# TensorE's order in the strand-only loops follows the kernel's rough clock

## The chip, the cores and the metric

The kernel runs on one core of one Trainium2 chip. The metric is the device time of one execution, in microseconds (us). The engines are named as the profile names them: PE is TensorE (PEld its weight loads), DVE is VectorE, ACT is ScalarE, POOL is GpSimd, SP is SyncE, whose queue issues most DMAs.

## What is computed

Two model blocks run one after the other on 512 latent tokens ("l") and 256 context tokens ("c") of width 1024, in float32. The part that the change touches is the first mixer, `mixer_ab`: a projection, a spatial gate, and a two-directional delta-rule scan over 8 heads of 64.

```python
def rwkv7_scan(r, w, k, v, kk, b, s0):
    def step(s, inp):
        r_t, w_t, k_t, v_t, kk_t, b_t = inp
        sa = jnp.einsum('bhvk,bhk->bhv', s, kk_t)
        s = s * w_t[:, :, None, :] - sa[..., None] * b_t[:, :, None, :] + v_t[..., None] * k_t[:, :, None, :]
        return s, jnp.einsum('bhvk,bhk->bhv', s, r_t)
...
def mixer_ab(hc, hl, ...):
    pc, pl = hc @ w_in, hl @ w_in
    bc, bl = rwkv_bidir(pc, pl, ...)            # both directions, context first
    yl = jnp.concatenate([spatial_gate(pl, a_ws, a_bs, a_gv), bl], axis=-1) @ w_out
    yc = jnp.concatenate([spatial_gate(pc, ...), bc], axis=-1) @ w_out
```

After it come a convolutional feed-forward, a second layer with an mLSTM mixer, and a second block of two hybrid layers (gated delta rule, long convolution, gates) with a last norm.

## The kernel before, in words

Activations lie with channels on the partitions. Large products are split into a high and a low part and done as three matmuls per 128 x 128 weight tile (`mmacc`: L331, L334, L335). The kernel is written for a scheduler that places every engine's instructions by a simulated time; what the kernel's text fixes on top of that is TensorE's order, by "pins".

**Strands.** The scans are Python generators, called strands. `background` adds one; each `yield a, b` says that the piece just written takes `a` ns of TensorE and that the strand can go on about `b` ns later. The kernel keeps a rough clock `now`, advanced by the `a` of every piece and by the matmuls of `mmacc`; a strand is due at `now + b * LF * slow` with LF = 2.5 (`step`). `tick` runs every strand that is due. So the text of the program comes out in the order of the rough clock.

**Pins.** `pin` orders a TensorE instruction behind the one pinned last, without a semaphore. `step` pins the first TensorE instruction of each strand step, and `mmacc` pins the first of its three matmuls while strands are there. A step's other TensorE instructions are not pinned.

**Where only strands run.** `finish(strands)` lets the strands run on, with no large matmul between, until the given ones are done (`wait` moves the rough clock to the next due time). Here the kernel before switches pins off, and forgets the last pinned instruction: the scheduler alone orders TensorE. There are two long such loops, both in `mixer_ab`. The first (`K.finish(early)`) follows `gate_part` and runs until head pairs 0 and 1 are done; pairs 2 and 3 (`rwkv_pair`, one strand per pair) and `ada` run beside them. The rough clock goes from 174 to 466 us there. Then `gemm_out` multiplies by `ab_w_out` with the remaining strands between its matmuls, and `K.drain()` is the second loop, for the last pairs: 532 to 602 us of the rough clock. `hybrid` has a `K.drain()` too, which finds two short steps left.

**Names.** L1025 are the LoRA products of `rwkv_prep` ("wd", then "ad"), L1122 its key products, L1144 the product behind them, L726 and L735 the two half-steps of `Chunk.inverse`, L1177 the products of `rwkv_scan`, L978, L979, L966, L971 those of `rwkv_end`. `ada` multiplies by the `ada_w` weights (L545), eight steps per round, one yield of 860 and 2800 each. The tail of `gate_part`, per segment, is L361 (column sums), L353 on POOL (the root), L375 (broadcast), L1258 on DVE, L1261 (transpose), L1263 on ACT, L1266 (the spatial product), L1269 and L1271 on DVE. PSUM has eight banks; the tail of `gate_part` and `ada` both use bank 3 alone.

Of the kernel before, what the change touches and what calls it, by code (L numbers as in the profile page):

```python
# [81 lines left out]
class Kern:  # L82
# [67 lines left out]

    def finish(self, strands):

        self.pinning, self.pinned = False, None
        while any(s in self.back for s in strands):
            self.wait()
        self.pinning = True

    def wait(self):
        self.now = max(self.now, min(s[2] for s in self.back))
# [2130 lines left out]
```

## Time and profile before

| | |
|---|---|
| median of 3 runs | 3410.71 us (3401.76 to 3412.95) |
| profiled execution | 3407.66 us, span 3406.0 us |
| PE busy | 3156.2 us, 93% of the span |
| DVE busy | 2114.3 us, 62% |
| ACT busy | 1271.8 us, 37% |
| mean granted PE clock | 0.958 |

PE is the busiest engine over the whole. Busy time of PE counts a matmul up to its modelled end, so that short waits between matmuls don't show as idle. The two strand-only loops are short stretches: by the instructions that belong to them, the first has its TensorE work between 374.6 and 711.4 us, the second between 804.7 and 847.8 us of the span.

### The profile page before, as it was taken

What the parts mean: (1) busy time and instruction counts of PE and PEld (TensorE: products, weight loads), DVE (VectorE), ACT (ScalarE), POOL (GpSimd) and SP (SyncE); (2) the same over time, 40 slices, a digit from 0 to 9 for tenths busy, and PEclk for the clock granted to TensorE, in tenths of its full rate; (3) what the DMA queues carried; (4) which work ended last, traced back from release to release, by engine and by line L of the source; (5) the groups of instructions that cost most, each with busy time, mean ns of one, the idle gap of its engine ahead of it and who ended that gap; (6) DMA issues with size and microseconds to landing.
All of it is one profiled execution on the core that took longest, in us unless ns stands there. A gap on an engine that the chain in (4) does not pass through costs nothing. (4 is left out here: it accounts for less than half of the span.)

```text
span 3406.0 us, 61963 instructions
## 1 busy us (share of the span) xinstructions
PE 3156.2 (93%) x25042; PEld 2473.4 (73%) x25042; DVE 2114.3 (62%) x4318; ACT 1271.8 (37%) x2681; POOL 624.0 (18%) x762
## 2 busy tenths in 40 slices
PE   7999988889899999989888999989999998899998
PEld 4878766667588888868766788857667676766756
DVE  4444556545855555584766675668578666777765
ACT  4333333333432222355534332352333335244332
POOL 4111223211000000010010000005158100515700
PEclk9999999999899999989999999989999898999989
DMA  7432545441222122222222233232223253223333
GB/s 233 137 94 71 166 148 166 133 124 51 76 72 69 64 79 66 77 66 71 87 66 87 87 100 123 87 100 72 72 90 100 76 174 95 75 69 100 100 118 105
DMA packets 313570, 336.10 MB, mean 99 GB/s; under 512 B 26542, under 2 KB 259132, under 8 KB 313284
## 3 DMA queue, kind: packets, MB, share of 16 engines
q1 hardware_dynamic: 311172, 329.69, 30.6%
q8 instruction: 197, 3.23, 0.4%
q0 software_dynamic: 2112, 2.45, 0.3%
q14 instruction: 89, 0.73, 0.1%
HBM read 282.13 MB, written 49.94 MB: 97 GB/s over the span
## 5 line engine op out<-in xcount | busy, mean ns | idle before, releaser
L331 PE MATMUL mm<-hl,wh 128*128 128x512 f32 (+1 forms) x3296 | 1252.2, 384 | 53.8 <-DVE qkv L1779 13.8
L334 PE MATMUL mm<-hl,wh 128*128 128x512 f32 (+1 forms) x3296 | 1223.6, 372 | 1.9 <-DVE hl L474 1.6
L335 PE MATMUL mm<-hl,wl 128*128 128x512 f32 (+1 forms) x3296 | 1215.9, 371 | 0.0
L331 PEld LDWEIGHTS mm<-hl,wh 128*128 128x128 f32 x3296 | 629.6, 192 | 194.8 <-issue 40.4
L335 PEld LDWEIGHTS mm<-hl,wl 128*128 128x128 f32 x3296 | 630.3, 191 | 114.0 <-issue 2.3
L334 PEld LDWEIGHTS mm<-hl,wh 128*128 128x128 f32 x3296 | 632.2, 192 | 104.9 <-DVE hl L474 4.0
L77 ACT ACTIVATE wh<-wr 128x512 fp32r<-128x512 f32 (+3 forms) x718 | 367.4, 561 | 698.1 <-PE mm L334 610.9
L78 DVE TENSOR_TENSOR wl<-wr,wh 128x512 fp32r<-128x512 f32 (+3 forms) x718 | 438.3, 644 | 213.6 <-ACT wh L77 196.8
L1357 DVE SCALAR_TENSOR_TENSOR cv<-mm,vecs,cv 128x441 f32<-128x441 f32 (+2 forms) x352 | 243.0, 692 | 94.2 <-ACT cv L1345 88.1
L1408 POOL MEMSET gwh<- 128x1024 f32 x3 | 2.9, 955 | 971.3 <-PE mm L334 971.3
L1779 DVE SCALAR_TENSOR_TENSOR cfa<-ld,vecs,cfa 128x497 f32<-128x497 f32 (+14 forms) x160 | 154.3, 964 | 18.3 <-ACT cfa L1773 16.1
L1945 POOL TENSOR_SCALAR tap<-ld,vecs 128x498 f32<-128x498 f32 (+4 forms) x80 | 150.7, 1883 | 46.7 <-DVE kq L2004 10.4
L1380 DVE TENSOR_TENSOR fy<-fy,mm 128x512 f32<-128x512 f32 x96 | 55.1, 576 | 126.3 <-PE mm L335 125.5
L1946 POOL TENSOR_TENSOR cfa<-cfa,tap 128x498 f32<-128x498 f32 (+4 forms) x80 | 113.0, 1413 | 5.3
L2121 ACT ACTIVATE u<-ps,beT 64x128 f32<-64x128 f32 x128 | 46.3, 362 | 137.1 <-DVE u L2120 136.1
L730 ACT ACTIVATE pad<-ps 128x256 f32<-128x256 f32 (+1 forms) x100 | 46.6, 467 | 129.9 <-PE ps L726 129.4
L1359 ACT ACTIVATE cv<-cv,vecs 128x256 f32<-128x256 f32 (+1 forms) x66 | 43.0, 653 | 132.1 <-DVE cv L1357 77.2
L736 DVE TENSOR_TENSOR cut<-cut,ps 128x256 f32<-128x256 f32 x120 | 49.4, 413 | 58.9 <-PE ps L735 57.2
L353 POOL TENSOR_TENSOR rs<-var,mhalf 128x4 f32<-128x4 f32 (+1 forms) x26 | 28.1, 1082 | 287.5 <-DVE var L351 287.4
L412 PE MATMUL ps<-sq,one 128*128 128x512 f32 (+1 forms) x132 | 64.5, 625 | 17.0 <-ACT sq L382 15.7
L1363 DVE TENSOR_TENSOR cv<-cv,mm 128x512 f32<-128x512 f32 x66 | 39.4, 599 | 65.5 <-ACT cv L1359 36.2
L2120 DVE TENSOR_SCALAR u<-ps,kdT 64x128 f32<-64x128 f32 x128 | 44.6, 348 | 52.9 <-PE ps L2116 44.5
(479 smaller groups left out, 4465.3 us busy)
## 6 DMA issues: line engine op xcount, KB each, us to landing
ar<-in_ada_w_dram SPq DMA_DIRECT2D x96, 512.0 KB
wr<-in_ffn_up_dram SPq DMA_DIRECT2D x44, 1024.0 KB
wr<-in_w_in_dram SPq DMA_DIRECT2D x28, 1024.0 KB
ld<-sp SPq DMA_DIRECT2D x84, 256.0 KB
wr<-in_w_in_dram SPq DMA_DIRECT2D x32, 512.0 KB
xsp<-x SPq DMA_DIRECT2D x48, 256.0 KB
x<-xsp SPq DMA_DIRECT2D x48, 256.0 KB
wr<-in_ffn_down_dram SPq DMA_DIRECT2D x20, 512.0 KB
```

Of the source, the lines that this page charges most:

```text
L77: nc.scalar.activation(h[:, q:e], src, AF.Copy)
L78: nc.vector.tensor_tensor(l[:, q:e], src, h[:, q:e].bitcast(F32), SUB)
L331: mm = nc.tensor.matmul(ps[:m, :n], wh[:, i, :m], H[:, :n], start=first and i == 0, stop=False)
L334: nc.tensor.matmul(ps[:m, :n], wh[:, i, :m], L[:, :n], start=False, stop=False)
L335: nc.tensor.matmul(ps[:m, :n], wl[:, i, :m], H[:, :n], start=False, stop=last and i == nk - 1)
L412: self.nc.tensor.matmul(ps[:, :n], self.one2, t[:, :n], start=first, stop=last)
L736: nc.vector.tensor_tensor(Wp, Wp, ps, SUB)
L1357: nc.vector.scalar_tensor_tensor(t3[:, ro, co], a3[:, ri, ci], tap(ky, kx, ff), t3[:, ro, co], MUL, ADD)
L1380: nc.vector.tensor_tensor(y[s][q], y[s][q], pss[s][:, :n], ADD)
L1779: nc.vector.scalar_tensor_tensor(dst[:, a:b], src[:, a + o:b + o], taps[j], dst[:, a:b], MUL, ADD)
L1945: nc.gpsimd.tensor_scalar(x[:, a:b], src[:, a + o:b + o], taps[j], None, MUL)
L1946: nc.gpsimd.tensor_tensor(g[:, a:b], g[:, a:b], x[:, a:b], ADD)
```

## The change

The two lines that switch pins off and on in `finish` go. Pins then hold in the strand-only loops as they do elsewhere, and the last pinned instruction is kept across the call: the first step in the loop stands behind the last pinned matmul ahead of it, and the first matmul of `gemm_out` behind the last step of the loop.

```diff
     def finish(self, strands):
 
-        self.pinning, self.pinned = False, None
         while any(s in self.back for s in strands):
             self.wait()
-        self.pinning = True
 
     def wait(self):
```

Line numbers below `finish` are two lower in the changed kernel (L545 is L543, L966 is L964, and so on). What the kernel computes, and the text order of its instructions, stay the same. What moves is the place of instructions on the engines.

The first place is TensorE at the start of the first loop, in the kernel before. L361, L375, L1261, L1266 are the tail of `gate_part`, the rest are strand steps; ps_4259 is `ada`'s first bank.

```order
L361 MATMUL ps_4185<-ones_77,sq_4183 128x1 x2
L726 MATMUL ps_4267<-cut_1168,pad_1296 64x64 x8
L726 MATMUL ps_4279<-cut_1543,pad_1644 64x64 x8
L735 MATMUL ps_4291<-pad_1295,bk_3503 64x64 x8
L1177 MATMUL ps_4311<-cut_1163,rk_3652 64x64
```

Sixty rows on, still of the kernel before, `ada` begins, with three of its steps in one piece:

```order
L1177 MATMUL ps_4831<-cut_1538,cut_1542 64x64 x4
L545 MATMUL ps_4259<-ar_4260,csil_341 32x512 x4
L545 MATMUL ps_4259<-ar_4330,csil_341 32x512 x4
L545 MATMUL ps_4259<-ar_4506,csil_341 32x512 x2
L545 MATMUL ps_4259<-ar_4507,csil_341 32x512 x2
```

TensorE at the same place in the changed kernel:

```order
L373 MATMUL ps_4194<-ident_72,rs_4192 128x128 x4
L1259 MATMUL ps_4200<-ident_72,gv_4025 128x128 x4
L1264 MATMUL ps_4207<-wsT_2624,gvt_4205 128x128 x4
L359 MATMUL ps_4220<-ones_77,sq_4218 128x1 x2
L1023 MATMUL ps_4359<-wd_665,up_4337 64x128 x2
L373 MATMUL ps_4227<-ident_72,rs_4225 128x128 x2
L1023 MATMUL ps_4427<-ad_725,up_4337 64x128 x2
L1259 MATMUL ps_4231<-ident_72,gv_4027 128x128 x2
L1264 MATMUL ps_4236<-wsT_2624,gvt_4234 128x128 x2
L543 MATMUL ps_4259<-ar_4260,csil_341 32x512 x4
L724 MATMUL ps_4267<-cut_1168,pad_1296 64x64 x8
L724 MATMUL ps_4279<-cut_1543,pad_1644 64x64 x8
```

The strand steps that stood between the parts of the tail now stand behind `ada`'s first step, and that one behind the whole tail, whose bank it takes.

The second place is TensorE inside the first loop, around an end step of pair 1 (`rwkv_end`: ps_7303, then ps_7346), in the kernel before:

```order
L978 MATMUL ps_7303<-y_1291,heads_87 128x256
L979 MATMUL ps_7303<-bon_1293,heads_87 128x256
L545 MATMUL ps_6451<-ar_7309,csil_341 32x512 x4
L735 MATMUL ps_7336<-cut_4243,bk_6603 64x64 x2
L726 MATMUL ps_7353<-cut_4256,cut_4252 64x64 x8
L966 MATMUL ps_7346<-blk_83,bon_1293 128x2 x2
```

And in the changed kernel:

```order
L976 MATMUL ps_7303<-y_1291,heads_87 128x256
L977 MATMUL ps_7303<-bon_1293,heads_87 128x256
L543 MATMUL ps_6451<-ar_7309,csil_341 32x512 x4
L733 MATMUL ps_7316<-cut_4251,bk_6816 64x64 x8
L733 MATMUL ps_7326<-pad_1643,bk_6422 64x64 x8
L733 MATMUL ps_7336<-cut_4243,bk_6603 64x64 x8
L964 MATMUL ps_7346<-blk_83,bon_1293 128x2 x2
```

One `ada` step and two pieces of other strands' half-steps stood between ps_7303 and ps_7346; now one `ada` step and three whole half-steps do.

## Rows read from the trace of the kernel before

**Rows 1.** The page's first line, of the whole execution.

```profile
span 3406.0 us, 61963 instructions
```

**Rows 2.** Stretches: length, busy PE, PEld, DVE, ACT, POOL, clock, DMA share, GB/s.

```profile
374.67:397.08 22.41, 18.45 (x366) 15.09 (x365) 12.99 (x36) 11.89 (x35) 6.36 (x12) 0.93 0.41 121
397.08:711.40 314.32, 274.06 (x5551) 207.23 (x5551) 190.06 (x486) 117.45 (x359) 88.11 (x157) 0.92 0.51 163
804.70:851.20 46.50, 37.99 (x655) 29.94 (x655) 27.82 (x73) 13.88 (x40) 10.96 (x15) 0.93 0.07 21
110.00:374.00 264.00, 263.92 (x2991) 213.66 (x2990) 119.69 (x266) 100.80 (x227) 49.32 (x88) 1.00 0.33 100
```

**Rows 3.** Timeline of PE, start of the first loop: start, length, instruction, idle before.

```profile
374.17 0.50 PE L361 MATMUL ps<-ones,sq 128*128 128x1 f32 x4
...
376.82 0.65 PE L375 MATMUL ps<-ident,rs 128*128 128x128 f32 x4
...
378.48 0.66 PE L1261 MATMUL ps<-ident,gv 128*128 128x128 f32 x4
...
380.67 1.16 PE L1266 MATMUL ps<-wsT,gvt 128*128 128x128 f32 x8
...
382.75 0.61 PE L361 MATMUL ps<-ones,sq 128*128 128x1 f32 x4
...
387.92 0.43 PE L375 MATMUL ps<-ident,rs 128*128 128x128 f32 x2
...
389.83 0.44 PE L1261 MATMUL ps<-ident,gv 128*128 128x128 f32 x2
...
393.52 0.85 PE L1266 MATMUL ps<-wsT,gvt 128*128 128x128 f32 x4 [2.59 <-ACT gvt L1263]
...
397.08 4.59 PE L545 MATMUL ps<-ar,csil 128*32 128x512 f32 x24
```

**Rows 4.** Timelines of POOL, DVE and ACT around the same tail.

```profile
374.95 1.01 POOL L353 TENSOR_TENSOR rs<-var,mhalf 128x4 f32<-128x4 f32 x1 [2.54 <-DVE var L351]
397.70 0.61 POOL L914 DMA_DIRECT2D up<-in_b_w_up_dram  x1 [3.44 <-DVE gv L1271]
377.58 0.75 DVE L1258 SCALAR_TENSOR_TENSOR gv<-gv,vecs,ps 128x512 f32<-128x512 f32 x1 [0.60 <-PE ps L375]
381.87 0.69 DVE L1269 TENSOR_TENSOR gv<-ps,bs 128x512 f32<-128x512 f32 x1 [1.07 <-PE ps L1266]
395.32 0.41 DVE L1269 TENSOR_TENSOR gv<-ps,bs 128x256 f32<-128x256 f32 x1
379.18 0.60 ACT L1263 ACTIVATE gvt<-ps 128x512 f32<-128x512 f32 x1 [0.54 <-PE ps L1261]
```

**Rows 5.** Waits of PE, 397.2 to 702 us: total, times, longest.

```profile
PE ps L735 <- ACT cut L730: 4.8, 3, 3.6
PE ps L966 <- ACT bon L981: 3.0, 1, 3.0
PE ps L1177 <- DVE cut L1196: 2.8, 3, 2.1
...
PE ps L1025 <- ACT cut L1027: 1.9, 4, 1.0
PE ps L1177 <- ACT Pb L1191: 1.8, 2, 1.4
```

**Rows 6.** Timelines of PE and ACT: a LoRA pair in the first loop.

```profile
386.86 0.45 PE L1025 MATMUL ps<-wd,up 64*64 64x128 f32 x8 [0.67 <-DMA up<-in_b_w_up_dram]
387.36 0.62 ACT L1027 ACTIVATE cut<-ps,hv 128x128 f32<-128x128 f32 x2 [0.84 <-PE ps L1025]
```

**Rows 7.** Timeline of PE: an end step, and what stands inside it.

```profile
574.73 0.70 PE L978 MATMUL ps<-y,heads 128*128 128x256 f32 x2 [1.22 <-ACT cut L1027]
...
576.95 0.63 PE L726 MATMUL ps<-cut,cut 64*64 64x64 f32 x16
580.59 0.61 PE L966 MATMUL ps<-blk,bon 128*128 128x2 f32 x4 [3.01 <-ACT bon L981]
```

## The prediction

> **What bounds the kernel now.** I read the page first: one core, a span of 3406.0 us [rows 1], and PE as the engine that is nearly always busy. Then the stretches. Where large matmuls run beside strands, PE has no idle time at all: 263.92 of 264.00 us busy, at the full granted clock [rows 2]. There pins can only change which work comes first. In the two strand-only loops this is different. From 397.08 to 711.40 us PE is busy for 274.06 of 314.32 us, so 40.3 us are idle, and the clock is 0.92; from 804.70 to 851.20 us it is 37.99 of 46.50 us, so 8.5 us idle at 0.93 [rows 2]. DVE is at 190 of 314 us and ACT at 117, so no engine is full: four strands and `ada` share PE, each waits for its own chain over DVE and ACT, and PE waits when the next instruction in its order isn't ready. The list of waits shows how that is made up: no wait is frequent, each kind comes one to four times with at most 3.6 us [rows 5]. The reader is to see that the change has some 360 us to act on, a tenth of the span, that about 49 us of it are idle PE, and that everything outside can only shift.
>
> What the change does there is to replace one fixed order by another. PE takes its instructions in order in both kernels; no strand can overtake at run time. The question is which order guesses better when a step is ready: the scheduler's simulated time, or the rough clock with its waits of 2.5 times the written latency.
>
> **The change part by part.**
>
> *Start of the first loop.* `ada`'s first step needs bank 3, which the tail of `gate_part` holds until DVE's L1269 has read it, at 395.32 + 0.41 = 395.73 us [rows 4]; `ada` starts at 397.08 [rows 3]. Before, strand steps fill that time. After, the first pinned step of the loop is `ada`'s, and every strand step stands behind it. Between the end of L361 (374.17 + 0.50 = 374.67) and 397.08 PE is busy for 18.45 of 22.41 us [rows 2]; the tail's own pieces are 0.65 + 0.66 + 1.16 + 0.61 + 0.43 + 0.44 + 0.85 = 4.80 [rows 3], so 13.65 us are strand work that moves behind `ada`. But the tail gets quicker when it is alone. Its first half is 0.28 until the root on POOL starts, 1.01 for the root, 0.65 on PE, 0.75 DVE, 0.66 PE, 0.60 ACT, 1.16 PE, 0.69 DVE = 5.80 [rows 3, 4]; the second half, with the first half's durations where no row of its own stands, 0.61 + 0.28 + 1.01 + 0.43 + 0.75 + 0.44 + 0.60 + 0.85 + 0.41 = 5.38. With some 14 hand-offs of about 0.1 (L1261 starts 0.15 after DVE's L1258 ends, ACT's L1263 0.04 after L1261) that is 12.6 us, so `ada` starts near 387.3, 9.8 us sooner, with 13.65 us undone: **+3.9**. The bounds are +13.65 (the tail as slow as now) and 0 (the moved work falls into later idle time). Moved along with it are the weights of pair 3: POOL issues them once the tail's last DVE step has freed their page, at 397.70 [rows 4]; they come sooner by the same 10 us, and no queue is behind in a way that costs.
>
> *The clock there.* A mean of 0.93 over 22.41 us is 14% of the time at the lower of the two levels, 3.1 us [rows 2]. PE will be mostly idle for 12 us, so I expect one more such stretch behind it; half of its work is lost: **+1.6**, bounds 0 and +5.
>
> *LoRA pairs.* From the first "wd" product (386.86) to the end of ACT's tanh (387.36 + 0.62 = 387.98), on which "ad" waits for its bank, 1.12 us pass [rows 6]. The rough clock gives about the same, 0.25 + 0.3 * 2.5 = 1.0 to 1.15 us, in which the changed order has about one piece of another strand, 0.6 us long as the half-step at 576.95 [rows 7]. Sixteen such pairs stand in the loop: 16 * 0.5 = 8.0, less the 1.9 us that PE waits there today [rows 5]: **+6.1**, bounds 0 and +8.
>
> *End steps.* Here the rough clock guesses better. L978 to L966 took 5.86 us, with PE idle for 3.01 at the end [rows 7]. Before, one `ada` step and part of two half-steps stand inside; after, `ada` and three half-steps, about 1 us more of cover. That makes the 3.0 us some 2, and a little at the other five end steps: **-2**, bounds -4 and +2.
>
> *Scan and inverse steps.* In the scan PE waits in five rows, from 2.8 to 1.8 us, 11.5 in all [rows 5]. The rough clock allows 1.6 to 2.0 us for a step, and the order before had put what it took to be ready between them. I take a third more: **+4**. The bounds are wide, since neither order knows how long DVE's queue is: all of 11.5 us gone, or as much again. The inverse half-steps (4.8 us of waits on ACT in three, nearly all one case of 3.6 [rows 5]) I leave as they are, 0.
>
> *The second loop* has 8.5 us idle [rows 2] and two or three strands whose rough waits are all too long by the same factor, so that their order among each other hardly moves: **+1**, bounds -4 and +4. *The joint with `gemm_out`*: its first matmul now stands behind the loop's last step. That is the step that makes its last operand, so I take 0, at most +3. *The drains in `hybrid`* hold two short steps: 0.
>
> The sum is 3.9 + 1.6 + 6.1 - 2 + 4 + 1 = +14.6 us. Against its own time the profiled execution goes from 3407.66 to 3422.3 us; it lies 3.05 us below the median of the runs shown, 3410.71, so the median would be 3425.3. I forecast 3425. A later end of the first loop passes on in full, since behind it stands work that keeps PE full.
>
> **The rivals.** *Faster: the rough clock covers waits better.* Its waits are 2.5 times the written latency, so it puts more work between two steps of a strand than a scheduler that trusts its own shorter times. L966 speaks for it [rows 7]; LoRA pairs and the start speak against. If half of the 40.3 idle us goes, that is -20. With it goes clock: 0.92 over 314.32 us is 16%, 50 us at the lower level, which costs 25 us of work; half of that back is -12. With +3.9 at the start: -28, 3383 us. The Trainium skill (Perfetto Trace Analysis, Matmul Optimizations) says that matmuls should be issued back to back in batches since the engine's clock goes with its use; the changed order does have longer batches, with each step's matmuls less mixed with those of others. The trace agrees in that the full stretch has 1.00 and the loops 0.92 and 0.93 [rows 2]; by that rule alone the 25 us would come back, 3386 us.
>
> *No change.* The idle time moves, its sum doesn't: strands wait for DVE and ACT whatever PE's order, and the start costs 4 us. That gives 3405 to 3420, say 3413. For it speaks that no kind of wait dominates [rows 5]. It is also what would come if the pins changed too little, since a pin holds only the first matmul of a step.
>
> *Much slower: blocked behind DVE's queue.* One wait of 3.6 us shows what happens when ACT or DVE is late and PE's next piece needs it [rows 5]. The scheduler's order hides most such cases by mixing steps; with pins in step order the whole of PE stands. If this comes once in each of some 15 blocks of 128 tokens in the loop, with 2.5 us, that is +37, with the 14.6 above +52: 3462 us. It decides where the delay is longer than the two or three pieces, about 2 us, that stand between.
>
> **How the numbers follow.** The forecast gets 0.42, the faster case 0.18, no change 0.28, much slower 0.12. A measurement of this kernel can tell about 0.3%, 10 us, from no change. Of the forecast's 0.42 a part of 0.08 lies under 10 us. So faster 0.17 (0.01 of the faster case is too small to see), same 0.28 + 0.08 + 0.01 = 0.37, slower 0.34 + 0.12 = 0.46. The forecast alone has 3413 to 3445. The range for eight in ten must reach into both ends: 3388 to 3460.
>
> **What would show it.** The first L543 of `ada` near 387 us with PE idle around the tail of `gate_part`, and strand steps only behind it: the first term. Waits of L1023 on ACT's tanh, short and about sixteen: the third. A shorter wait at L964: the fourth. Idle PE time of the first loop of 50 us or more against 44 says slower, under 30 says faster, and the clock in it goes the same way. The stretches of `gemm_out` and behind the mixer should keep their length; if they change by more than 5 us, something moved that I don't see. The forecast is wrong if DVE's or ACT's order changes so that strands get their results sooner: then all waits shrink together.

## The result and the profile after

The changed kernel takes 3454.94 us (median, 3450.47 to 3464.73), the kernel before beside it 3411.83 us: a ratio of 1.0134 with a 95% interval of 1.0117 to 1.015, that is 43 us more. I had forecast 3425, so the sign was right and the size a third of what came. The first profiled execution of the changed kernel lies 9.8 us above its median. A second one, beside the experiments, took 3450.58 us (median there 3451.28, ratio 1.0128, 1.011 to 1.0146), and all readings below are of that one unless another is named. It stands 42.9 us above the profiled execution of before.

The stretches of the changed kernel, with the columns of [rows 2]: the tail of `gate_part` from the end of its column sums to `ada`'s first product, the first loop, `gemm_out`, the second loop, and all that follows.

```profile
375.21:391.15 15.94, 8.66 (x37) 5.93 (x36) 3.36 (x7) 1.86 (x5) 2.89 (x4) 0.59 0.36 114
391.15:743.40 352.25, 298.83 (x5857) 228.70 (x5857) 199.45 (x514) 132.08 (x392) 90.51 (x167) 0.87 0.48 147
743.40:839.20 95.80, 91.92 (x1015) 71.57 (x1014) 34.49 (x88) 28.27 (x77) 12.31 (x20) 0.96 0.30 90
840.10:887.40 47.30, 39.41 (x652) 33.13 (x650) 25.75 (x66) 13.07 (x38) 11.19 (x15) 0.85 0.06 19
887.40:3440.20 2552.80, 2387.49 (x14012) 1873.52 (x14010) 1678.61 (x3259) 952.65 (x1851) 412.92 (x336) 0.96 0.28 87
```

The last three of these in the kernel before:

```profile
711.40:803.90 92.50, 88.10 (x1000) 68.82 (x997) 34.78 (x88) 29.51 (x81) 13.18 (x21) 0.96 0.29 89
804.70:847.80 43.10, 36.85 (x652) 29.24 (x651) 25.33 (x66) 13.25 (x39) 10.96 (x15) 0.96 0.07 23
847.80:3397.70 2549.90, 2385.63 (x14010) 1874.80 (x14010) 1678.75 (x3259) 952.94 (x1851) 411.23 (x336) 0.96 0.28 87
```

| stretch | before | after | difference | predicted |
|---|---|---|---|---|
| tail of `gate_part` | 22.41 | 15.94 | -6.5 | -9.8 |
| first loop | 314.32 | 352.25 | +37.9 | +23.4 |
| `gemm_out` | 92.50 | 95.80 | +3.3 | 0 |
| second loop | 43.10 | 47.30 | +4.2 | +1 |
| behind | 2549.90 | 2552.80 | +2.9 | 0 |

(The predicted 23.4 of the first loop is the 13.65 us of moved work, 1.6 of clock, and 6.1 - 2 + 4.) Tail and loop together are 31.5 us longer. PE is busy for 8.66 + 298.83 = 307.49 us in them against 18.45 + 274.06 = 292.51 [rows 2], 15.0 more for the same instructions, and idle for 60.7 against 44.2, 16.5 more. The granted clock of the loop is 0.87 where it was 0.92.

The tail, PE's timeline (columns as in [rows 3]):

```profile
376.56 0.65 PE L373 MATMUL ps<-ident,rs 128*128 128x128 f32 x4 [1.35 <-POOL rs L351]
378.12 1.11 PE L1259 MATMUL ps<-ident,gv 128*128 128x128 f32 x4 [0.91 <-DVE gv L1256]
379.92 2.07 PE L1264 MATMUL ps<-wsT,gvt 128*128 128x128 f32 x8 [0.69 <-ACT gvt L1261]
382.78 1.01 PE L359 MATMUL ps<-ones,sq 128*128 128x1 f32 x4 [0.78 <-DVE gv L1267]
386.36 0.69 PE L1023 MATMUL ps<-wd,up 64*64 64x128 f32 x4 [2.57 <-DMA up<-in_b_w_up_dram]
...
391.15 1.94 PE L543 MATMUL ps<-ar,csil 128*32 128x512 f32 x8 [0.52 <-DVE gv L1267]
393.02 1.97 PE L724 MATMUL ps<-cut,pad 64*64 64x64 f32 x32
```

The waits that I had listed are there, and `ada` does stand behind the tail, with nearly all strand steps behind it. Two things are new against [rows 3]. The pieces take nearly twice as long (L1264 2.07 us for 1.16), since the clock is at the lower of its two levels through most of it. And a LoRA step of pair 2, L1023, waits 2.57 us for its weights in the middle of the tail, with the tail's second half behind it in PE's order. POOL issues these weights only behind the second segment's column sums (L359), and that segment's root (L351) stands behind the issues, as POOL's timeline shows:

```profile
384.09 0.62 POOL L912 DMA_DIRECT2D up<-in_b_w_up_dram  x1 [7.58 <-PE ps L359]
...
385.26 0.72 POOL L351 TENSOR_TENSOR rs<-var,mhalf 128x2 f32<-128x2 f32 x1
```

In the kernel before the same product starts at 386.86, also behind a wait for the weights [rows 6], but strand steps fill most of the time ahead of it.

PE's waits in the first loop (total, times, longest), which answer to [rows 5]:

```profile
PE ps L733 <- ACT cut L728: 7.9, 4, 5.5
PE ps L724 <- DVE cut L734: 7.3, 6, 2.8
PE ps L1023 <- ACT cut L1025: 7.0, 7, 3.5
PE ps L1120 <- DVE kq L1101: 6.2, 4, 1.9
PE ps L1175 <- DVE cut L1194: 4.7, 4, 3.2
PE ps L724 <- ACT cut L1151: 4.2, 1, 4.2
PE ps L1175 <- DVE cut L1207: 4.1, 4, 1.5
PE ps L964 <- ACT cut L979: 2.0, 1, 2.0
PE ps L1175 <- DVE cut L734: 1.8, 1, 1.8
PE ps L1175 <- ACT cut L1193: 1.4, 2, 0.9
```

Two rows of the kernel before that [rows 5] left out, of the same list over 397 to 711.4 us:

```profile
PE ps L726 <- DVE cut L736: 2.3, 3, 1.3
...
PE ps L1122 <- DVE kq L1103: 1.7, 3, 1.1
```

So these two rows of waits for DVE, on L734 (its L736) and on L1101 (its L1103), grew from 4.0 to 13.5 us. All waits for DVE in the two lists grew less, from 19.4 to 25.6 us, those for ACT from 17.3 to 25.9, and the longest ones are for ACT. Two of them show how PE comes to stand. Before 424.95 PE waits for L734, which DVE takes up only when it is through with a row of one block's `rwkv_prep` work, of which the last is L1101; before 709.80 it waits for L728, which stands in ACT's queue behind a reload of `gemm_out` that hasn't landed (DVE's timeline, and PE's):

```profile
423.18 1.29 DVE L1101 TENSOR_TENSOR kq<-kq,cut 128x256 f32<-128x256 f32 x2
424.39 0.41 DVE L734 TENSOR_TENSOR cut<-cut,ps 128x256 f32<-128x256 f32 x1
```

```profile
424.95 0.62 PE L724 MATMUL ps<-cut,pad 64*64 64x64 f32 x14 [2.81 <-DVE cut L734]
...
709.80 1.12 PE L733 MATMUL ps<-cut,bk 64*64 64x64 f32 x16 [5.53 <-ACT cut L728]
```

ACT's timeline ahead of the second:

```profile
708.40 1.08 ACT L309 ACTIVATE hl<-ld 128x512 fp32r<-128x512 f32 x2 [4.71 <-DMA ld<-sp]
709.39 0.36 ACT L728 ACTIVATE cut<-ps 128x256 f32<-128x256 f32 x1
```

These waits look like the answer. But the experiments that took some of them away gained little.

### The profile page after: what moved, and what is told of

The parts are those of the page before. It is cut to its first block, busy times and chain, and to the rows that moved or that the text cites. A ratio compares the mean times of both kernels' runs of the same rounds, so it can differ in the third digit from the quotient of the medians.

```text
span 3463.0 us, 61943 instructions
## 1 busy us (share of the span) xinstructions
PE 3192.6 (92%) x25042; PEld 2498.9 (72%) x25042; DVE 2113.3 (61%) x4318; ACT 1275.6 (37%) x2681; POOL 625.0 (18%) x762
## 5 line engine op out<-in xcount | busy, mean ns | idle before, releaser
L728 ACT ACTIVATE pad<-ps 128x256 f32<-128x256 f32 (+1 forms) x100 | 46.6, 467 | 139.5 <-PE ps L724 137.9
L734 DVE TENSOR_TENSOR cut<-cut,ps 128x256 f32<-128x256 f32 x120 | 49.2, 413 | 61.7 <-PE ps L733 60.5
L351 POOL TENSOR_TENSOR rs<-var,mhalf 128x4 f32<-128x4 f32 (+1 forms) x26 | 28.9, 1111 | 290.5 <-DVE var L349 290.4
```

The costliest lines, as they stand in the source:

```text
L734: nc.vector.tensor_tensor(Wp, Wp, ps, SUB)
```

## The experiments

The changed kernel again, for the second profile used above:

> The changed kernel once more, for a second profile of it (the first one's execution lies 9.8 us above its median). Theory (the 9.5 us by which the work behind the mixer was longer in the first profile belong to that execution, not to the change): behind the second loop the two kernels take the same time within 3 us, and loop 1 ends 30 to 36 us later than in the kernel before; 3455 us. Rival (the change also lengthens what comes behind the mixer): 5 us or more are lost there again.

Behind the second loop it takes 2552.80 us against 2549.90, 2.9 more. The first profile had lost some 10 us there, of which 7 were that execution's own.

**Which loop.** Pins in the first loop only, and in the second only:

```diff
     def drain(self):
 
+        self.pinning, self.pinned = False, None
         self.finish(list(self.back))
+        self.pinning = True
```

> Pins stay on in the first strand-only loop and are off in K.drain(), as in the kernel before. Theory (the first loop carries the loss: start, waits, and more time at the lower clock): its loop 1 ends as in the changed kernel, near 749 us of the span, gemm_out keeps its 97 us, the second loop goes back from 47 to about 43 us: 3450 us, +39 on the kernel before. Rival (the second loop's own order costs nothing; what it lost it inherits from the first, by DVE and ACT work that is late): the second loop stays at 47 us, 3455 us. Second rival (the loss is spread evenly by idle time, 40 us in the first loop to 8.5 in the second): 3412 + 43 * 40/49 = 3447 us.

```diff
+    K.pinning, K.pinned = False, None
     K.finish(early)
+    K.pinning = True
```

> Pins are off in the first strand-only loop, as in the kernel before, and stay on in K.drain(). Theory (first loop carries the loss): loop 1 ends near 711 us and gemm_out takes 92.5 us as in the kernel before, the second loop takes 47 us for 43: 3416 us. Rival (the second loop's extra time is inherited from the first): 3412 us, second loop 43 us. Second rival (spread evenly by idle time): 3412 + 43 * 8.5/49 = 3419 us.

The first loop alone gives 3449.95 us, a ratio of 1.011 (1.0093 to 1.0128), +39; the second alone 3411.72, 1.0009 (0.9998 to 1.0019), no difference that can be told. Its interval ends at +6.5 us, though, and its profile has 46.9 us for the second loop against 43.1, so a cost of some 4 us isn't excluded. The loss is made in the first loop, or at its ends.

**The start.** `ada`'s steps without pins, so that strand steps may stand between the parts of the tail again:

```diff
-            if i.engine == mybir.EngineType.PE and self.pinning:
+            if i.engine == mybir.EngineType.PE and self.pinning and s[1].__name__ != "ada":
```

> Pins stay on, but the steps of ada are not pinned, so that strand steps of the first loop may again stand between the parts of gate_part's tail; the rest of TensorE's order hardly differs from the changed kernel. Theory (the start cost 6.8 us of displaced work and some 2 of clock): ada's first product near 398 us with some 13 us of strand work ahead of it, loop 1 ends near 740 us for 749, 3446 us. Rival (the displaced work would fall into idle time of the loop anyway, so giving it back early only lengthens later waits): first product near 398 us too, loop 1 ends near 749 us, 3453 to 3455 us. By the price in the prediction, 3.9 + 1.6, it would be 3449 us.

It took 3431.57 us, 1.0057 (1.0041 to 1.0073). That is 20 to 23 us less than the changed kernel, where the theory of that day said 9. And the work that came back into the tail is small: PE is busy there for 10.90 us instead of 8.66. `ada`'s first product comes at 392.50 and not near 398, since the LoRA step of pair 2 still stands in the tail, with a wait of 3.12 us for its weights, and the steps that follow are held behind it. Its stretches from 375.00 us to `ada`'s first product, and from there to the end of the loop:

```profile
375.00:392.50 17.50, 10.90 (x143) 8.11 (x141) 5.22 (x13) 6.15 (x15) 4.51 (x7) 0.81 0.41 122
392.50:727.00 334.50, 288.70 (x5767) 220.86 (x5767) 197.28 (x509) 127.12 (x383) 87.66 (x163) 0.90 0.49 153
```

With some 2 us more of PE work in the tail the loop ends 16.4 us earlier (727.0 for 743.4). The amount of work alone can't have done that. But `ada`'s later steps are free here too, so this run doesn't show the start by itself. The reverse experiment does. It keeps the pins of the first 12 strand steps (the 13th switches them off) and leaves the rest to the scheduler:

```diff
     def finish(self, strands):
 
-        self.pinning, self.pinned = False, None
+        if not self.first:
+            self.pinning, self.pinned = False, None
...
+        if self.first:
+            self.first -= 1
+            if not self.first:
+                self.pinning, self.pinned = False, None
         self.env, self.busy = s[0], True
...
+    K.first = 13
     K.finish(early)
```

> The kernel before, with pins kept across the first 13 strand steps of the first loop and switched off behind them: TensorE's order round gate_part's tail is that of the changed kernel, the rest is left to the scheduler. Theory (holding ada's first step behind the tail is itself worth about half of the 43 us, as the 23 us say that came back when ada's steps were not pinned): first product of ada near 392 us, the lower clock in the tail and behind it, loop 1 ends 15 to 23 us later than in the kernel before, 3428 to 3434 us. Rival 1 (the price in the prediction, 3.9 + 1.6): 3416 us. Rival 2 (only the work displaced, 7 us and 2 of clock; the rest of the 23 came from waits at the end of the loop that fell otherwise): 3420 us.

3433.53 us, 1.008 (1.0057 to 1.0103): 24 us from the start alone, four times the 5.5 of the prediction (3.9 and 1.6 for the clock). The tail and the loop:

```profile
375.82:391.40 15.58, 8.19 (x36) 5.63 (x37) 3.36 (x7) 1.86 (x5) 2.90 (x4) 0.63 0.37 117
391.40:734.70 343.30, 293.16 (x5870) 226.18 (x5870) 199.50 (x512) 129.01 (x390) 92.57 (x165) 0.89 0.48 150
```

Moved work of 13.65 us less 6.8 of a shorter tail would leave +7; tail and loop together are 358.88 us against 336.73, +22, with an order behind the start that the scheduler chose freely. So what is lost in the start isn't made up in the 340 us behind it, although PE is idle for 50 of them.

**The clock at the start.** PE's idle time in the tail filled with matmuls that nobody reads, each group pinned behind the piece of the tail ahead of it:

```diff
+                def fill(m):
+                    for d in warm:
+                        K.pin(next(i for i in reversed(nc.cur_bb.bb.instructions) if i.engine == mybir.EngineType.PE))
+                        for _ in range(m):
+                            K.pin(nc.tensor.matmul(d, X["c"][0][0][:, :P], X["l"][0][0], start=True, stop=True).ins)
```

> The changed kernel with 35 more matmuls of 128x512 that nobody reads, put into TensorE's idle time in gate_part's last tail (5, 4, 3, 3 in its first half, 10, 4, 3, 3 in its second), each group behind the piece of the tail that stands ahead of the gap. What is computed is the same. Theory (the clock falls because TensorE is idle in the tail, and the tail's own pieces and the first work behind it then run at half speed): the granted clock of 376 to 397 us rises from 0.6 to near 1, ada's first product comes 1 to 3 us sooner, and the loop begins at full clock: 3446 to 3451 us. Rival (the clock there does not go with TensorE's own work, or the fall comes later all the same): the same clock or another stretch of the same length, and the filler only lies in the way, 3455 to 3460 us.

3442.81 us, 1.0102 (1.0085 to 1.0118), 8 to 12 us less than the changed kernel although PE does 35 matmuls more; its slowest run, 3447.53 us, lies below the fastest of the changed kernel, 3450.11. The tail, the loop, and a part of the loop near its start:

```profile
376.09:390.47 14.38, 13.35 (x73) 9.12 (x72) 3.35 (x8) 1.85 (x5) 2.89 (x4) 1.00 0.39 120
390.47:733.80 343.33, 292.51 (x5857) 223.57 (x5856) 199.52 (x514) 131.07 (x392) 91.24 (x168) 0.89 0.49 151
402.70:412.90 10.20, 9.42 (x114) 6.56 (x111) 6.61 (x20) 2.43 (x9) 1.18 (x6) 0.50 0.46 143
```

PE's timeline, a piece of the tail (L1278 here, L1264 in the changed kernel) at full speed:

```profile
380.35 1.16 PE L1278 MATMUL ps<-wsT,gvt 128*128 128x128 f32 x8
```

With PE busy for 13.35 of 14.38 us the clock stays at 1.00; with 8.66 of 15.94 it is 0.59. So the clock follows what PE did in the tail. But the lower level isn't gone with the filler: it comes behind the tail, for 10.2 us from 402.70, where the changed kernel has it for 17 us from 378.10 and the kernel before for 6.9 us from 393.90. The rival was half right in that the fall comes later; the stretch is shorter. The loop ends at 733.80, 9.6 us earlier than in the changed kernel.

**Other ways out.** The reloads of `gemm_out` split on POOL instead of ACT and DVE:

```diff
-            K.split(t, *X[s][k])
+            H, L = X[s][k]
+            K.nc.gpsimd.tensor_copy(H, t)
+            K.nc.gpsimd.tensor_tensor(L, t, H.bitcast(F32), SUB)
```

> The changed kernel with the split of gemm_out's reloaded operands (L309 on ACT, L310 on DVE) done on POOL, so that ACT and DVE don't stand behind a reload that has not landed. Theory (the two longest waits of TensorE in loop 1, 7.0 us at 716.65 and 3.8 us at 742.23, come from ACT's queue standing at gemm_out's loads: 6.1 us at a reload, 4.4 us at a weight slab): the wait of 7.0 us at L733 goes, that of 3.8 stays since the weight slab's split is still on ACT; 3455 - 7 - 1 to 3 of clock = 3445 to 3447 us. Rival (the strands are late at that place for another reason and the next wait takes its place): L733 or its successor still waits 5 us or more there, 3452 to 3456 us. If POOL is too slow for twelve splits and gemm_out starts later: above 3456 us.

3450.27 us, 1.0111 (1.0086 to 1.0136), 1 to 5 us less, not the 8 to 10 of the theory, and inside what the intervals allow for no change. The wait at L733 went. At the same place PE now waits 3.3 us for POOL's L716, and this is POOL's timeline there:

```profile
707.59 0.61 POOL L1286 CAST hl<-ld 128x512 fp32r<-128x512 f32 x1 [3.74 <-DMA ld<-sp]
...
709.05 0.72 POOL L716 TENSOR_TENSOR cut<-cut,zm 128x256 f32<-128x256 f32 x1
```

POOL makes the masks of the half-steps (L716), and now they stand behind the same late load. Which queue waits for the load was changed, not that strands stand behind it.

The next three start from the kernel with `ada` unpinned (3431.57) and try to mend the rough clock. Factor 4.0 for 2.5 in the loops; a longer written wait between the LoRA products; a long row of DVE work cut in three:

```diff
-        s[2] = self.now + r[1] * LF * s[3]
+        s[2] = self.now + r[1] * self.lf * s[3]
...
+        self.lf = 4.0
         while any(s in self.back for s in strands):
             self.wait()
+        self.lf = LF
```

> The kernel whose ada steps are not pinned, with the factor on the written waits 4.0 for 2.5 inside the two strand-only loops. Theory (TensorE waits there since the rough clock puts a step too early, ahead of the DVE or ACT result that it needs): more work between two steps of a strand, waits of TensorE in loop 1 fall from 46 us to 30 or 35 and the clock rises with them, 3412 to 3420 us. Rival (all due times move by the same factor and the order among strands hardly changes): within 5 us of 3431.6. A loss, above 3437 us, if ada, whose steps come more rarely or in longer rows, is left over at the end of the loop.

```diff
-    yield 250, 300
+    yield 250, K.lora    # 900 in the strand-only loops
     BK = K.p2(name="bk")
```

> The kernel whose ada steps are not pinned, with the written wait between the wd and the ad product 900 ns for 300 inside the two strand-only loops (2.25 us of the rough clock for 0.75). Theory (the LoRA waits, 7.4 us of L1023 on ACT's tanh in seven waits, come from the rough clock's short wait): these waits fall under 3 us, 3425 us with a little clock. Rival (ACT's tanh stands in ACT's queue behind other strands' work, so that a step put later meets another late result): the sum of all waits in loop 1 stays near 46 us, within 3 us of 3431.6.

```diff
     nc.vector.tensor_tensor(kd, kI, iD, MUL)
 
+    if K.loop:
+        yield 0, 400
     loc_at = [o for _, o in loc]
...
+    if K.loop:
+        yield 0, 400
     for t, m in ((kk, skew(0, S + 1, C64)), (r, skew(1, S - 1, C64))):
```

> The kernel whose ada steps are not pinned, with rwkv_prep's long row of DVE work behind the ad product (some ten instructions, 4.2 us) cut into three pieces by two yields without TensorE work, inside the two strand-only loops. Theory (TensorE, held to its order, stands at L724 since DVE works off that whole row before the half-step's L734: 7.3 us in six waits, 2.8 the longest): another strand's L734 gets between the pieces, the waits of L724 on L734 fall under 4 us, loop 1 shortens by 3 to 6 us, 3425 to 3429 us. Rival (DVE's order is set by the simulated time and not by the order of the text, so the row stays in one piece, or L1120 then waits longer for the last of it): waits of loop 1 in sum within 2 us of 46, 3430 to 3435 us.

They took 3449.94 (ratio to before 1.0119, 1.0101 to 1.0136), 3441.08 (1.0096, 1.0078 to 1.0113) and 3433.55 us (1.007, 1.0053 to 1.0088), where the theories had 3412 to 3420, 3425, and 3425 to 3429: worse than 3431.57, worse, and the same. The second is the clearest. Its waits in the first loop that matter here (its line numbers are two above those of the list that follows) are

```profile
PE ps L1177 <- DVE cut L1209: 9.8, 6, 3.0
PE ps L726 <- DVE cut L736: 8.3, 6, 2.9
...
PE ps L1025 <- ACT cut L1027: 4.0, 6, 1.1
```

and those that they answer to, with `ada` unpinned and the old wait:

```profile
PE ps L1023 <- ACT cut L1025: 7.4, 7, 3.1
PE ps L724 <- DVE cut L734: 7.3, 6, 2.8
PE ps L1175 <- DVE cut L1207: 5.7, 5, 2.0
```

The LoRA waits fell from 7.4 to 4.0 us, others rose by as much, and the loop ends where it had, at 727.2 us for 727.0. In the two profiles the time is lost behind the loop: from its end to the second loop 99.4 us pass for 94.5, and the second loop takes 52.5 us, at a clock of 0.73, for 45.3 at 0.96 (what follows is 7.2 us shorter in this profile). Few strands are left there to fill a longer wait; that this is the reason isn't shown. Cutting DVE's row made the longest wait of its kind 2.2 us for 2.8 and left the sum (7.2 for 7.3). PE's whole idle time in the loop, 45.8 us, went up in all three, to 50.0 here, 52.1 with the cut row and 55.5 with the factor. None of the three bears out the theory that PE stands because the rough clock is too quick.

**Pins from the 40th step on.** Nearly the complement of the start alone; steps 13 to 39 are free in both:

```diff
+        self.free_steps -= 1
+        if not self.free_steps:
+            self.pinning, self.pinned = True, None
         self.env, self.busy = s[0], True
...
+    K.pinning, K.pinned, K.free_steps = False, None, 40
     K.finish(early)
```

> The changed kernel with pins off for the first 40 strand steps of the first loop, so that its start is ordered as in the kernel before, and on from there. Theory (the strands are chains of their own; what the changed kernel loses is above all that all of them are held at the start, by 18 to 20 us when TensorE reaches the same work near 420 us, and by 11 to 14 us where only ada is left unpinned, since the LoRA step that waits for its weights still stands ahead of the others; the pins of the later loop cost what the delay grows by behind that, 4 to 17 us, and gemm_out and the second loop 7): delay near 0 at 420 us, loop 1 ends 4 to 14 us later than in the kernel before, 3421 us, between 3416 and 3430. Rival (what is lost at the start is only TensorE work and would be made up, pins cost all along the loop): the delay grows steadily, 3431 to 3440 us, no better than with ada alone unpinned.

3439.36 us, 1.0088 (1.0069 to 1.0107), +30. My theory missed here: with the start as in the kernel before I had expected +11. The start alone costs 24, the rest alone 30, both together 43. Where the two overlap is seen when the same PE instruction is looked up by its name in each pair of traces. The table has the medians of these delays, over the steps of a strand that start in the stretch (times of the kernel before), and how much later the loop ends.

| kernel | pair 0, 374-382 | pair 0, 420-440 | pair 0, 560-600 | pair 3, 420-440 | loop's end |
|---|---|---|---|---|---|
| changed | +20.2 | +23.0 | +31.7 | +8.7 | +32.0 |
| start alone | +21.0 | +22.1 | +20.2 | +9.0 | +23.3 |
| `ada` unpinned | +10.1 | +16.7 | +21.3 | +2.2 | +15.6 |
| pins from step 40 | +2.1 | +14.8 | +19.4 | -0.7 | +18.0 |
| tail filled | +17.9 | +21.8 | +25.1 | +5.9 | +22.4 |

In every one of them pair 0 is 15 to 23 us late within the first 65 us of the loop, most of what it is at the end. From there to the loop's end the delay changes little, by +1 us with the start alone and with the tail filled, +3 with the late pins and -1 with `ada` unpinned; in the changed kernel it grows by 9. With the late pins the delay arises in one step, where they come on. Pair 0's first key product of the loop (L1122 before, L1124 there, L1120 in the changed kernel), in PE's timeline of the kernel before:

```profile
406.39 0.34 PE L1122 MATMUL ps<-kq,bk 64*64 64x128 f32 x3
```

With late pins:

```profile
427.97 1.23 PE L1124 MATMUL ps<-kq,bk 64*64 64x128 f32 x14
```

In the changed kernel:

```profile
436.42 1.04 PE L1120 MATMUL ps<-kq,bk 64*64 64x128 f32 x15
```

Its predecessor, the "ad" product, stands at 389.2 us in the kernel before and at 390.4 with late pins. The scheduler had let pairs 0 and 1 run ahead as soon as they were ready. The rough clock puts pairs 2 and 3 and `ada` in turn with them: in its order 47 steps of the loop stand ahead of that product. It even slows pairs 0 and 1: `mixer_ab` sets their factor `slow` to 1.2 ahead of the loop (`SLO`), while pairs 2 and 3 and `ada` have 1.0. At 420 to 440 us pair 3 isn't late at all with the late pins, and pair 0 is, by 14.8; the loop, which waits for pairs 0 and 1 alone, ends 18.0 us later. The lead can be lost once, by being held behind the tail or by taking turns, which would explain why the two prices don't add up. The lead isn't the whole of it, though. Looked up in the same way, at 560 to 600 us all four pairs are late by the same: 19 us with the late pins, 20 with the start alone, 31 to 32 in the changed kernel.

What this leaves open: that the end hangs on the chains of pairs 0 and 1 is read from the early delays and from what `finish(early)` waits for, and isn't shown, since pairs 2 and 3 are as late by 560 us. A rough clock that gives these two pairs their lead back, with pins on, was not tried.

**Filler elsewhere.** The filled tail pointed to a version that might beat both kernels: the kernel before, with filler in PE's waits of the large norms.

```diff
+        self.fill(12, n)
-        return self.bcast_rows(r, n)
+        rb = self.bcast_rows(r, n)
+        self.fill(8, n)
+        return rb
```

> The kernel before (pins off in the loops), with 20 matmuls of 128x128 that nobody reads in each of the nine large norms of the 512 tokens: 12 behind L412's sums, where TensorE waits some 2.4 us for POOL's root, and 8 behind L375's broadcast, where it waits 1.5 to 2.8 us for ACT. What is computed is the same. Theory (as in gate_part's tail: TensorE idle between short pieces brings the lower clock, and filler keeps it up): of the 54 us at the lower clock round the norms a third to a half goes, 27 us of work, so -8 to -14 us: 3397 to 3403 us. Rival (filler covers too little of each norm, the waits for ACT's squares stay open): the same stretches stay at the lower clock and the filler costs what it covers no wait of, 3410 to 3416 us.

3427.20 us, 1.0042 (1.0028 to 1.0056), slower by 16 where the theory had 8 to 14 less. The norm behind the second loop, from the end of the products ahead of it to the first product behind it, with filler:

```profile
871.90:907.87 35.97, 27.55 (x132) 18.15 (x131) 26.27 (x68) 13.22 (x25) 5.06 (x8) 0.95 0.28 100
```

The same in the kernel before:

```profile
865.90:896.40 30.50, 21.88 (x52) 9.84 (x51) 24.57 (x67) 12.61 (x25) 5.06 (x8) 0.72 0.33 114
```

The clock rose from 0.72 to 0.95 and the norm took 5.5 us longer all the same. DVE is busy for 24.57 of the 30.50 us of the kernel before, so PE's speed can hardly be on the path there. Filler is, where the scheduler put it ahead of a sum (L412), as in PE's timeline with filler (L436):

```profile
877.41 4.42 PE L436 MATMUL mm<-ident 128*128 128x128 f32 x24
881.66 1.88 PE L412 MATMUL ps<-sq,one 128*128 128x512 f32 x4
```

None of the versions beats the kernel before.

## Why the prediction was right in sign and short in size

*Start of the first loop, +3.9: the step that failed.* I valued the hold by the PE work that it moves, 13.65 us, less the time that the tail gains. That would be right where PE is the bound. Here PE is idle for 40 of 314 us [rows 2], and the strands, which begin 18 us later (393.02 for the 374.6 of before), are still late at the loop's end. Alone the start measured +24, for 5.5 with the clock's term. I had the row in hand that says so, the idle PE, and used it only for the rivals.

*The tail alone, 12.6 us.* It took 15.94, so `ada` began at 391.15 and not near 387. The lower clock is about half of the 3.3 us: with the tail filled and the clock at 1.00 it still took 14.38. The rest comes with a step that I had put behind `ada`: pair 2's LoRA step is inside the tail and waits until 386.36 for its weights, and the second segment's root starts 1.47 us behind its column sums instead of 0.28. The order shown with the change and [rows 6] had both the step and its wait, and my sum left them out.

*The clock, +1.6.* Far too small. Filling the tail gave 8 to 12 us back, and the loop's clock went from 0.92 to 0.87, to which I had given nothing. I put the 15.0 us of longer PE time in tail and loop down to it, since the instructions are the same; no run shows that by itself.

*LoRA pairs, +6.1.* Nearly as large as forecast: 7.0 us of waits against 8.0, 5.1 more than before, in seven waits and not sixteen. But taking 3.4 us of them away, in the kernel with `ada` unpinned, moved the loop's end by 0.2. The term was the right size for a wait, and there it didn't lie on the path.

*End steps, -2.* L964's waits are 2.0 and 0.9 us in both profiles of the changed kernel against 3.0 and 1.4, -1.5, as reasoned. *Scan, +4.* Too large: the four rows of L1175 above and two small ones come to 12.6 us, for 11.5 before. *Inverse half-steps, 0.* Mis-sized: L733 and L724 wait 7.9 + 7.3 + 4.2 us, where [rows 5] and the row of L726 above have 4.8 and 2.3. I had called the one 3.6 us wait a single case. There too ACT's queue stood at a late load (3.56 us at its L311, until 675.36), and that came again, longer.

*Second loop, +1, and the joint, 0.* 4.2 and 3.3 us in the profile; by its own run the second loop's order costs nothing that can be told. *Behind: unchanged,* 2.9 us in 2550, as said.

*The rivals.* The time came out at that of "blocked behind DVE's queue", 3462, for half of its reason. Such waits exist, 2.8 us at 424.95, but not once per block, and cutting DVE's row left their sum as it was. That the range reached up to 3460 it owes to this rival's share; that it held the time was luck as far as the mechanism goes. "Faster" had the clock going up with longer batches, with the Trainium skill (Perfetto Trace Analysis, Matmul Optimizations) behind it, which has the engine scale power by its utilization. The trace agrees in that the granted clock of the tail goes with PE's use (1.00 with the tail filled, 0.59 without). It doesn't bear out what I made of it: the changed order keeps a step's matmuls together, and the loop's clock fell, with PE idle for 60.7 us in tail and loop against 44.2.

## What to carry over

Where an engine has idle time, price a change of its order by which chain of work gets later, and whether the end waits for that chain, not by the work that is moved. Look first at the hand-over into such a stretch: a delay made in its first 65 us was still there at its end, while waits that were shortened inside it were replaced by others. Look there, too, at what else stands in the queues, here a step that waits for its weights. Filler that kept the clock up paid in the tail, and cost time in a norm where DVE was the busier engine.

## What the runs showed of the hardware

In the tail the clock fell to its lower level although no wait of PE there had been longer than 1.35 us: from 375.21 us to the fall PE was busy for 0.66 of 2.89 us, in the 17 us behind it the granted clock was 0.50.

```profile
375.21:378.10 2.89, 0.66 (x5) 0.41 (x4) 0.91 (x2) 0.15 (x1) 1.01 (x1) 0.99 0.42 74
378.10:395.10 17.00, 11.95 (x78) 7.80 (x80) 2.88 (x6) 2.16 (x6) 2.99 (x5) 0.50 0.40 128
```

It was not raised when PE was busy again at 386 us but at 395. And 35 useless matmuls, 10.0 us of busy PE by their own rows, made a kernel 8 to 12 us quicker, although the clock then fell for 10.2 us behind the tail.
